# A hybrid attention block: when an attention step makes its rotation tables, applies its keys' weights, and how a sub-norm folds 1/64

## The chip, the cores and the metric

The kernel runs on one core of one Trainium2 chip. The metric is device time in microseconds (us), the median of several executions. TensorE (PE) multiplies matrices, VectorE (DVE) and ScalarE (ACT) do elementwise work, GpSimd (POOL) small elementwise work, and SyncE (SP) issues the DMAs. Each engine works through its own queue in order.

## The reference, cut to what matters

One layer over 2048 tokens: a root-mean-square norm, an input projection, three branches side by side (latent attention with 8 heads, differential attention, attention into 256 memory tokens), a gate and an output projection. The change touches the heads of the latent branch and the sub-norm of the differential branch:

```python
def mla_branch(...):
    q = (rms_norm(cq, q_norm_g) @ w_uq).reshape(b, s, MLA_HEADS, MLA_QK)
    kv = (rms_norm(ckv, kv_norm_g) @ w_ukv).reshape(b, s, MLA_HEADS, MLA_NOPE + MLA_V)
    k_nope, v = kv[..., :MLA_NOPE], kv[..., MLA_NOPE:]
    k = jnp.concatenate([k_nope, k_rope], axis=-1)
    q = rms_norm(q, qn_g)
    k = rms_norm(k, kn_g)
    q = jnp.concatenate([q[..., :MLA_NOPE], rope(q[..., MLA_NOPE:], pos)], axis=-1)
    k = jnp.concatenate([k[..., :MLA_NOPE], rope(k[..., MLA_NOPE:], pos)], axis=-1)
    ...
def diff_branch(...):
    ...
    o = rms_norm(o, subln_g) * (1.0 - lam_init)
```

Here `rms_norm(x, g)` is x / sqrt(mean(x²) + 1e-6) · g; a head of the latent branch has 64 plain and 32 rotated elements.

## The kernel before

The work is cut into steps of 512 tokens (four tiles of 128). There are 4 steps `m` (memory), 8 steps `d` (differential, two groups of heads) and 16 steps `a` (latent, four groups of two heads). Each step has a preparation, which runs while the steps before it still multiply, and its maps: scores on PE, an exponential on ACT (line 506), the rest of it in a second 16-bit part on DVE (`plo`, line 507), and three matmuls per tile with the values (lines 516, 518, 536). A loop at the end of the kernel (lines 1203 to 1238) emits preparations, maps, projections and output tiles by due times written out by hand and gives each piece a priority. A scheduler then fixes each engine's order when the program is built: it plays the program through with its own idea of durations, and whenever an engine is free it takes, of the instructions that are then ready, the one of best priority. A piece that is emitted late can so be placed early, where nothing better is ready. On the chip the order is fixed; an instruction that is not ready holds up all behind it on its engine.

The preparation of an `a` step is `prep_a` (lines 825 to 901). PE projects the latents; ACT copies queries (line 844) and keys (845) to SBUF. ACT squares the keys in two halves (853) and the queries (855), and DVE sums them (854, 857). POOL adds the shared key's sum (861), adds epsilon (97) and raises to -0.5 (101), for queries and keys at once: this is the root, `r`. POOL also rotates the 32 last elements of the queries in place (`rope_in_place`, lines 354 to 358), with tables of cosine and sine times the norm weight that `rope_tabs` makes (four POOL operations, lines 332 to 335) in a buffer of which there is one (`tag="rtab"`, `bufs=1`, line 328). It scales the rotated shared key (866). DVE multiplies the keys by the root (871) and by `g_n`, the product of the two norm weights (872), and the queries by the root (874). ACT and DVE split keys and queries in two 16-bit parts (880, 881 and 886, 887), and SP's queue sends them through transposing DMAs (882 to `kT`, 890 to `qB`). An estimate of the row maxima on PE follows (398), from which the final `qB` is made (899).

The sub-norm of the differential branch is `post_d` (lines 590 to 607). ACT squares eight groups with their sums (596); POOL adds epsilon, takes the root and multiplies by 1/64 (97, 101, 599); DVE multiplies `y` by it (602).

In the kernel before, `prep_a` emits its root and its products so:

```python
        V.reduce_sum(ss[:, 0, :], sq.rearrange(...), axis=AX.X)
        tb = rope_tabs(b, g_q[:, 64:96], nm)
        ...
        V.tensor_tensor(kn[..., 0:64], kn[..., 0:64], _bc(rk, 3, 64), ALU.mult)
        V.tensor_tensor(kn[..., 0:64], kn[..., 0:64], _bc(_bc(g_n, 1, 2), 1, 4), ALU.mult)
        yield 1.0
        V.tensor_tensor(q, q, _bc(rq, 3, 96), ALU.mult)
```

Of the kernel before, what the change touches and what calls it, by code (L numbers as in the profile page):

```python
# [15 lines left out]
AF = mybir.ActivationFunctionType  # L16
ALU = mybir.AluOpType
# [8 lines left out]
EPS = 1e-6  # L26
NEG = -1.0e30
WS = 64.0
# [4 lines left out]
def _bc(ap, axis, n):  # L33
    ap = ap.unsqueeze(axis)
    shape = list(ap.shape)
    shape[axis] = n
    return ap.broadcast_to(shape)
# [3 lines left out]
def hybrid_block(ctx: ExitStack, tc: tile.TileContext, x, mem, positions, norm_g, w_in, mla_q_norm_g,  # L41
# [3 lines left out]
    V, A, G, T, SP = nc.vector, nc.scalar, nc.gpsimd, nc.tensor, nc.sync  # L45
# [37 lines left out]
    def gain_row(src, n, name):  # L83
        t = cst.tile([P, n], F32, name=name)
        SP.dma_start(t, src.broadcast_to([P, n]))
        return t
# [1 line left out]
    gx = gain_cols(norm_g, NK, "gx", WS)  # L88
    gm = gain_cols(mem_norm_g, NK, "gm", WS, G)

    def rstd_of(ss, shape, name, tag="rstd"):
        r = sm.tile([P, 32 if tag == "rstd" else 8], F32, tag=tag, name=name)
        n = int(np.prod(shape))
        rv = r[:, 0:n]
        if len(shape) == 2:
            rv = rv.rearrange("p (a b) -> p a b", b=shape[1])
        G.tensor_scalar(rv, ss, EPS, None, ALU.add)
        m = mhalf
        if len(shape) == 2:
            m = m.unsqueeze(2)  # L100
        G.tensor_tensor(rv, rv, m.broadcast_to([P] + list(shape)), ALU.pow)  # L101
        return rv
# [96 lines left out]
    def new_qkv(name):  # L199
        return wk.tile([P, 4, 256], F32, tag="qkv", name=name, bufs=2)  # L200
# [103 lines left out]
    g_q = gain_row(mla_qn_g, 96, "g_q")  # L304
    g_k = gain_row(mla_kn_g, 96, "g_k")
    g_n = cst.tile([P, 64], F32, name="g_n")
# [19 lines left out]
    def rope_tabs(b, g, name):  # L326

        tb = wk.tile([P, 2, 4, 32], F32, tag="rtab", name=f"rt_{name}", bufs=1)
        c = cos_t[:, 4 * b:4 * b + 4, :]
        s = sin_t[:, 4 * b:4 * b + 4, :]  # L330
        g1, g2 = _bc(g[:, 0:16], 1, 4), _bc(g[:, 16:32], 1, 4)
        G.tensor_tensor(tb[:, 0, :, 0:16], c, g1, ALU.mult)
        G.tensor_tensor(tb[:, 0, :, 16:32], c, g2, ALU.mult)
        G.tensor_tensor(tb[:, 1, :, 0:16], s, g2, ALU.mult)
        G.tensor_tensor(tb[:, 1, :, 16:32], s, g1, ALU.mult)
        return tb
# [202 lines left out]
    def new_ys(ct, b):  # L539
        return wk.tile([P, 2, 4, P], F16, tag="ys", name=f"ys{ct}_{b}", bufs=1)  # L540
# [49 lines left out]
    def post_d(st, y):  # L590
        y8 = y.rearrange("p t h d -> p (t h) d")
        ss = sm.tile([P, 8], F32, tag="yss", name=f"yss_{st.name}")
        ys = new_ys(4 + st.g, st.b)
        sink = ys[:, 0].rearrange("p t k -> p (t k)")
        for i in range(8):
            A.activation(sink[:, 64 * i:64 * i + 64], y8[:, i, :], AF.Square, scale=1.0 / 8.0, accum_out=ss[:, i:i + 1])
        yield 1.0
        r = rstd_of(ss[:, 0:8], [8], f"yr_{st.name}", "rstd_y")
        G.tensor_scalar(r, r, 1.0 / WS, None, ALU.mult)
        yield 1.0  # L600
        yield 1.0
        V.tensor_tensor(y8, y8, _bc(r, 2, 64), ALU.mult)
        yield 1.0
        yf = y.rearrange("p t h d -> p t (h d)")
        V.tensor_tensor(yf, yf, st.z, ALU.mult)
        yield 1.0
        yield from finish(st, yf, 4 + st.g, ys)
# [216 lines left out]

    def prep_a(st):
        g, b, nm = st.g, st.b, st.name
        q = new_qkv(f"qkv_{nm}")[:, :, 0:192].rearrange("p t (h d) -> p t h d", d=96)
        knt = tmp4(f"kn_{nm}")
        kn = knt[:, 0:768].rearrange("p (t h d) -> p t h d", t=4, d=96)
        vt = new_v(b, nm)  # L830
        G.memset(vt[:, :, :, 64:65], WS)
        for t in range(4):
            ps = ps_p.tile([P, 512], F32, tag="pp", name="pp")
            q0, k0 = 192 * g, 256 * g
            first = True
            for c in range(2):
                for hx, hw in ((0, 0), (0, 1), (1, 0)):
                    T.matmul(ps[:, 0:192], lhsT=lat_q[b][:, t, hx, c, :], rhs=wuq[c][:, hw, q0:q0 + 192], start=first,
                             stop=False, skip_group_check=True)
                    first = False  # L840
            for i, (hx, hw) in enumerate(((0, 0), (0, 1), (1, 0))):
                T.matmul(ps[:, 192:448], lhsT=lat_kv[b // 2][:, b % 2, t, hx, :], rhs=wukv[0][:, hw, k0:k0 + 256],
                         start=False, stop=(i == 2), skip_group_check=True)
            A.activation(q[:, t], ps[:, 0:192].rearrange("p (h d) -> p h d", d=96), AF.Copy, scale=1.0 / WS)
            A.activation(kn[:, t, :, 0:64], ps[:, 192:320].rearrange("p (h d) -> p h d", d=64), AF.Copy, scale=1.0 / WS)
            put_v(vt[:, t], ps[:, 320:448].rearrange("p (h d) -> p h d", d=64))
            yield 1.6
        sqt = tmp4(f"sqq_{nm}")
        sq = sqt[:, 0:768].rearrange("p (t h d) -> p t h d", t=4, d=96)
        ss = sm.tile([P, 2, 8], F32, tag="ssa", name=f"ss_{nm}")  # L850
        for i, m in enumerate((sqt, knt)):
            sk = m[:, 768:1024].rearrange("p (t h d) -> p t h d", t=2, d=64)
            A.activation(sk, kn[:, 2 * i:2 * i + 2, :, 0:64], AF.Square, scale=1.0 / math.sqrt(96))
            V.reduce_sum(ss[:, 1, 4 * i:4 * i + 4], sk.rearrange("p t h d -> p (t h) d"), axis=AX.X)
        A.activation(sq, q, AF.Square, scale=1.0 / math.sqrt(96))
        yield 1.0
        V.reduce_sum(ss[:, 0, :], sq.rearrange("p t h d -> p (t h) d"), axis=AX.X)
        tb = rope_tabs(b, g_q[:, 64:96], nm)
        yield 1.0
        s4 = ss[:, 1, :].rearrange("p (t h) -> p t h", h=2)  # L860
        G.tensor_tensor(s4, s4, _bc(ss_kr[b], 2, 2), ALU.add)
        r = rstd_of(ss.rearrange("p a b -> p (a b)"), [16], f"r_{nm}")
        rq = r[:, 0:8].rearrange("p (t h) -> p t h", h=2)
        rk = r[:, 8:16].rearrange("p (t h) -> p t h", h=2)
        yield 1.0
        G.tensor_tensor(kn[..., 64:96], _bc(krot[b], 2, 2), _bc(rk, 3, 32), ALU.mult)
        rope_in_place(q[..., 64:96], tb, 2, G, sqt[:, 768:1024])
        yield 1.0
        yield 1.0
        yield 1.0  # L870
        V.tensor_tensor(kn[..., 0:64], kn[..., 0:64], _bc(rk, 3, 64), ALU.mult)
        V.tensor_tensor(kn[..., 0:64], kn[..., 0:64], _bc(_bc(g_n, 1, 2), 1, 4), ALU.mult)
        yield 1.0
        V.tensor_tensor(q, q, _bc(rq, 3, 96), ALU.mult)
        kT = bigt([P, 2, 4, 2, P], f"kT_{nm}") if b in AB else kvp.tile([P, 2, 4, 2, P], F16, tag="kT", name=f"kT_{nm}")
        st.qs, st.qB = [], []
        for h in range(2):
            ks = stack([P, 4, 2, P], f"ks{h}_{nm}")
            G.memset(ks[:, :, :, 96:128], MS)
            A.activation(ks[:, :, 0, 0:96], kn[:, :, h], AF.Copy)  # L880
            V.tensor_tensor(ks[:, :, 1, 0:96], kn[:, :, h], ks[:, :, 0, 0:96], ALU.subtract)
            SP.dma_start_transpose(kT[:, h].rearrange("p t l k -> p (t l) k"), ks.rearrange("p t l d -> p (t l d)"))
            yield 1.0
            qs = stack([P, 2, 4, P], f"qs{h}_{nm}")
            G.memset(qs[:, :, :, 96:128], 0.0)
            A.activation(qs[:, 0, :, 0:96], q[:, :, h], AF.Copy)
            V.tensor_tensor(qs[:, 1, :, 0:96], q[:, :, h], qs[:, 0, :, 0:96], ALU.subtract)
            st.qs.append(qs)
            st.qB.append(new_qb([P, 2, 4, P], f"qB{h}_{nm}"))
            SP.dma_start_transpose(st.qB[h].rearrange("p l t k -> p (l t) k"), qs.rearrange("p l t d -> p (l t d)"))  # L890
            yield 1.0
        st.kTs = st.prev.kTs + [kT] if b else [kT]
        st.Vs = st.prev.Vs + [vt] if b else [vt]
        yield 1.0
        yield 1.0
        for h in range(2):
            yield from est_block(st, h, 1, lambda m: st.qs[h][:, 0, :, 96], lambda m, t: st.qB[h][0:96, 0, t, :],
                                 lambda m, c, n: st.kTs[c][0:96, h, 0:n, 0, :])
            SP.dma_start_transpose(st.qB[h][:, 0], st.qs[h][:, 0].rearrange("p t d -> p (t d)"))
            ready.add((nm, h))  # L900
            yield 1.0
# [208 lines left out]
    for kind, ng in (("m", 1), ("d", 2), ("a", 4)):  # L1110
        for g in range(ng):
            for b in range(NB):
                st = Step()
# [149 lines left out]
```

## Time and profile before

| | us |
|---|---|
| median of 3 runs | 1380.5 (1380.03 to 1385.78) |
| the profiled execution, its own time | 1382.39 |
| span of the profiled execution (first to last instruction) | 1380.7 |
| mean granted clock of TensorE, share of full speed | 0.983 |

The profile is of one execution. A line of the view by groups gives an engine, the operation's output and inputs, how often it ran, its busy time in us, the mean of one in ns, and the idle time of the engine ahead of it with what ended that. In a timeline a bracket is the idle time of the engine ahead of an instruction and what released it. The view by stretches gives, for each stretch, each engine's busy us with its count of instructions, the granted clock, the share of the DMA engines and GB/s.

### The profile page before, as it was taken

What the parts mean: (1) busy time and instruction counts of PE and PEld (TensorE: products, weight loads), DVE (VectorE), ACT (ScalarE), POOL (GpSimd) and SP (SyncE); (2) the same over time, 40 slices, a digit from 0 to 9 for tenths busy, and PEclk for the clock granted to TensorE, in tenths of its full rate; (3) what the DMA queues carried; (4) which work ended last, traced back from release to release, by engine and by line L of the source; (5) the groups of instructions that cost most, each with busy time, mean ns of one, the idle gap of its engine ahead of it and who ended that gap; (6) DMA issues with size and microseconds to landing.
All of it is one profiled execution on the core that took longest, in us unless ns stands there. A gap on an engine that the chain in (4) does not pass through costs nothing.

```text
span 1380.7 us, 35076 instructions
## 1 busy us (share of the span) xinstructions
PE 1297.6 (94%) x13616; PEld 834.4 (60%) x13616; DVE 1113.6 (81%) x2649; ACT 902.8 (65%) x2163; POOL 353.4 (26%) x549
## 2 busy tenths in 40 slices
PE   5988999999999999999999999999998988999998
PEld 2443556667677767767776656656665665655554
DVE  4657888879888867888998888988898888986745
ACT  6656544687877646786986567766766777774521
POOL 2322132403052233113212233232353333200000
PEclk9999999999999999999999999999999999999999
DMA  7998844323113322447345275446535443275452
GB/s 229 199 210 179 183 109 98 59 59 87 42 24 71 78 38 56 78 115 190 118 98 142 55 147 146 104 93 157 117 70 123 124 96 64 43 149 157 138 192 69
DMA packets 294263, 155.53 MB, mean 113 GB/s; under 512 B 239952, under 2 KB 272848, under 8 KB 294096
## 3 DMA queue, kind: packets, MB, share of 16 engines
q1 hardware_dynamic: 294064, 153.29, 47.1%
q8 instruction: 106, 1.74, 0.5%
q14 instruction: 61, 0.50, 0.1%
q0 software_dynamic: 32, 0.00, 0.0%
HBM read 61.75 MB, written 34.34 MB: 70 GB/s over the span
## 4 chain that ended last, share of the span: by engine, by line
PE 53%; DVE 14%; DMA 10%; POOL 9%; ACT 8%; issue 5%; SPq 1%; ACTq 0%; POOLq 0%; DVEq 0%
PE pp L187 6%; PE pp L188 6%; PE pp L189 6%; PE pe L398 5%; DVE plo L507 4%; PE pv L518 3%; PE pv L516 3%; PE pv L536 3%; PE st L572 3%; PE pp L957 3%; PE pp L958 3%; PE pp L959 3%; POOL r_a L101 2%; PE st L916 2%; PE st L917 2%
## 5 line engine op out<-in xcount | busy, mean ns | idle before, releaser
L506 ACT ACTIVATE p<-st 128x512 f32<-128x512 f32 (+3 forms) x672 | 356.1, 550 | 178.0 <-PE st L918 72.2
L507 DVE TENSOR_TENSOR plo<-p 128x512 f16<-128x512 f32 (+3 forms) x672 | 405.6, 615 | 61.9 <-ACT p L506 58.7
L407 ACT ACTIVATE ec<-pe 128x512 bf16<-128x512 f32 (+3 forms) x384 | 197.6, 536 | 34.1 <-PE pe L400 15.2
L516 PEld LDWEIGHTS <-p 128*128 128x128 bf16 x2304 | 187.0, 99 | 49.3 <-issue 5.1
L518 PEld LDWEIGHTS <-p 128*128 128x128 bf16 x2304 | 173.8, 98 | 41.5 <-issue 4.4
L408 DVE TENSOR_TENSOR er<-er,ec 128x512 bf16<-128x512 bf16 (+3 forms) x384 | 141.0, 377 | 29.9 <-ACT ec L407 15.1
L404 ACT ACTIVATE er<-pe 128x512 bf16<-128x512 f32 x192 | 110.2, 606 | 44.2 <-DVE mx_d L413 14.1
L536 PEld LDWEIGHTS <-plo 128*128 128x128 f16 x2304 | 123.6, 98 | 24.0 <-DVE plo L507 8.6
L916 PE MATMUL st<-qB_a,kT_a 97*128 97x512 f16 (+1 forms) x320 | 112.6, 352 | 19.2 <-ACT p L506 14.3
L189 PEld LDWEIGHTS <-ht_x 128*128 128x128 f16 x896 | 87.8, 98 | 54.8 <-ACT ht_x L137 5.1
L188 PEld LDWEIGHTS <-ht_x 128*128 128x128 f16 x896 | 87.8, 98 | 50.2 <-issue 6.4
L572 PE MATMUL st<-qB_d,kT_d 97*128 97x512 f16 (+1 forms) x320 | 112.2, 355 | 6.0 <-DMA qB_d<-s_d 2.9
L516 PE MATMUL pv<-V_d,p 128*128 128x65 f16 x1088 | 116.4, 194 | 0.8 <-DVE y_d L579 0.8
L187 PEld LDWEIGHTS <-ht_x 128*128 128x128 f16 x896 | 87.8, 98 | 46.6 <-issue 2.9
L518 PE MATMUL pv<-V_d,p 128*128 128x64 f16 x1088 | 115.9, 196 | 0.0
L516 PE MATMUL pv<-V_a,p 128*128 128x65 f16 x1088 | 113.9, 194 | 0.4 <-DVE y_a L923 0.4
L518 PE MATMUL pv<-V_a,p 128*128 128x64 f16 x1088 | 113.2, 196 | 0.0
L917 PE MATMUL st<-qB_a,kT_a 96*128 96x512 f16 (+1 forms) x320 | 112.3, 351 | 0.0
L398 PE MATMUL pe<-kT_d,qB_d 96*128 96x512 f16 (+2 forms) x320 | 106.4, 351 | 6.0 <-ACT ec L407 3.5
L918 PE MATMUL st<-qB_a,kT_a 96*128 96x512 f16 (+1 forms) x320 | 111.6, 349 | 0.0
L398 PE MATMUL pe<-kT_a,qB_a 96*128 96x512 f16 (+2 forms) x320 | 102.4, 353 | 6.6 <-DMA qB_a<-qs_a 3.1
L189 PE MATMUL pp<-w_d,ht_x 128*128 128x512 f16 x256 | 97.0, 379 | 0.0
(294 smaller groups left out, 3356.1 us busy)
## 6 DMA issues: line engine op xcount, KB each, us to landing
xt_x<-in_x_dram SPq DMA_DIRECT2D x16, 512.0 KB, 4.6
xr<-in_x_dram SPq DMA_DIRECT2D x16, 512.0 KB, 3.7
part<-xr SPq DMA_DIRECT2D x16, 512.0 KB, 3.1
ysc<-yt SPq DMA_DIRECT2D x31, 256.0 KB, 2.1
yl<-ysc SPq DMA_DIRECT2D x15, 512.0 KB, 4.4
zsc<-zc SPq DMA_DIRECT2D x48, 128.0 KB, 2.2
xa<-part SPq DMA_DIRECT2D x12, 512.0 KB, 3.6
out_dram<-xa SPq DMA_DIRECT2D x12, 512.0 KB, 3.3
```

The lines of the kernel that those rows point to most:

```text
L187: T.matmul(ps[:, :n], lhsT=ht[:, 0, k], rhs=wt[:, 0, :n], start=(k == 0), stop=False)
L188: T.matmul(ps[:, :n], lhsT=ht[:, 0, k], rhs=wt[:, 1, :n], start=False, stop=False)
L189: T.matmul(ps[:, :n], lhsT=ht[:, 1, k], rhs=wt[:, 0, :n], start=False, stop=(k == NK - 1))
L398: T.matmul(ps[:, 0:n], lhsT=lhs(m, t), rhs=rhs(m, c, n // P), start=True, stop=c < b)
L407: A.activation(ec[:, 0:n], ps[:, 0:n], AF.Copy)
L408: V.tensor_tensor(er[:, t % 2, 0:n], er[:, t % 2, 0:n], ec[:, 0:n], ALU.max)
L506: A.activation(p32[:, :n], ps[:, :n], AF.Exp, scale=self.scale)
L507: V.tensor_tensor(plo[:, :n], p32[:, :n], phi[:, :n], ALU.subtract)
L516: T.matmul(pvv[:, t, 0:65], lhsT=phi[:, c], rhs=vt[:, 0:65], start=(j == 0 and t == 0), stop=False, skip_group_check=True)
L518: T.matmul(pvv[:, t, 0:64], lhsT=phi[:, c], rhs=vt[:, 65:129], start=False, stop=False, skip_group_check=True)
L536: last["pv"] = T.matmul(pvv[:, t, 0:65], lhsT=plo[:, c], rhs=vt[:, 0:65], start=False, stop=(j == self.njt - 1), skip_group_check=True)
L572: T.matmul(ps[:, :n], lhsT=st.kTs[j // 4][0:97, h, j % 4, m % 2, :], rhs=st.qB[h][0:97, t0:4, m % 2, :], start=True, stop=not diag)
```

## The change

A step `a` calls `rope_tabs` as its first act, ahead of its buffers and its projection, where it stood behind the sum of the queries' squares. The product of the keys with `g_n` moves from behind their product with the root to the place that the tables leave, behind the sum of the queries' squares; both products are made in place, so the keys come out the same. (`if 1:` is always taken.) In the sub-norm ACT squares 64/8·y where it squared 1/8·y, epsilon is multiplied by 64² and the operation of line 599 goes: the power -0.5 of 64²·(mean + epsilon) is 1/64 of the root.

```diff
-    def rstd_of(ss, shape, name, tag="rstd"):
+    def rstd_of(ss, shape, name, tag="rstd", eps=EPS):
...
-        G.tensor_scalar(rv, ss, EPS, None, ALU.add)
+        G.tensor_scalar(rv, ss, eps, None, ALU.add)
...
-            A.activation(sink[:, 64 * i:64 * i + 64], y8[:, i, :], AF.Square, scale=1.0 / 8.0, accum_out=ss[:, i:i + 1])
-        yield 1.0
-        r = rstd_of(ss[:, 0:8], [8], f"yr_{st.name}", "rstd_y")
-        G.tensor_scalar(r, r, 1.0 / WS, None, ALU.mult)
+            A.activation(sink[:, 64 * i:64 * i + 64], y8[:, i, :], AF.Square, scale=WS / 8.0, accum_out=ss[:, i:i + 1])
+        yield 1.0
+        r = rstd_of(ss[:, 0:8], [8], f"yr_{st.name}", "rstd_y", EPS * WS * WS)
...
     def prep_a(st):
         g, b, nm = st.g, st.b, st.name
+        tb = rope_tabs(b, g_q[:, 64:96], nm)
...
         V.reduce_sum(ss[:, 0, :], sq.rearrange("p t h d -> p (t h) d"), axis=AX.X)
-        tb = rope_tabs(b, g_q[:, 64:96], nm)
+        V.tensor_tensor(kn[..., 0:64], kn[..., 0:64], _bc(_bc(g_n, 1, 2), 1, 4), ALU.mult)
...
-        V.tensor_tensor(kn[..., 0:64], kn[..., 0:64], _bc(rk, 3, 64), ALU.mult)
-        V.tensor_tensor(kn[..., 0:64], kn[..., 0:64], _bc(_bc(g_n, 1, 2), 1, 4), ALU.mult)
-        yield 1.0
-        V.tensor_tensor(q, q, _bc(rq, 3, 96), ALU.mult)
+        if 1:
+            V.tensor_tensor(kn[..., 0:64], kn[..., 0:64], _bc(rk, 3, 64), ALU.mult)
+        yield 1.0
+        if 1:
+            V.tensor_tensor(q, q, _bc(rq, 3, 96), ALU.mult)
```

## Rows read from the trace of the kernel before

**Rows 1.** The page's first part: busy time of each engine, its share, instructions

```profile
PE 1297.6 (94%) x13616; PEld 834.4 (60%) x13616; DVE 1113.6 (81%) x2649; ACT 902.8 (65%) x2163; POOL 353.4 (26%) x549
```

**Rows 2.** View by stretches: length, busy us per engine, clock, DMA share, GB/s

```profile
400.00:640.00 240.00, 231.25 (x2699) 165.86 (x2697) 197.54 (x513) 165.56 (x433) 73.81 (x101) 0.99 0.35 77
...
680.00:1245.00 565.00, 529.46 (x6086) 350.02 (x6083) 496.11 (x1182) 399.36 (x979) 175.76 (x285) 0.97 0.48 108
```

**Rows 3.** Waits of PE, 640 to 1245 us: total, times, longest

```profile
PE st L916 <- ACT p L506: 14.3, 14, 4.3
...
PE st L916 <- DMA qB_a<-qs_a: 4.2, 3, 2.1
...
PE pv L536 <- DVE plo L507: 3.3, 4, 1.5
...
PE pe L398 <- DMA qB_a<-qs_a: 3.1, 1, 3.1
```

**Rows 4.** Waits of DVE, whole span: total, times, longest

```profile
DVE kn_a L871 <- POOL r_a L101: 16.2, 10, 4.3
...
DVE y_d L602 <- POOL yr_d L599: 6.9, 7, 2.7
```

**Rows 5.** Timeline of DVE at the longest wait: start, length

```profile
1058.66 0.69 DVE L871 TENSOR_TENSOR kn_a<-kn_a,r_a 128x512 f32<-128x512 f32 x1 [4.28 <-POOL r_a L101]
1059.27 1.37 DVE L874 TENSOR_TENSOR qkv_a<-qkv_a,r_a 128x768 f32<-128x768 f32 x1
1060.56 0.68 DVE L507 TENSOR_TENSOR plo<-p 128x512 f16<-128x512 f32 x1
1061.16 0.68 DVE L872 TENSOR_TENSOR kn_a<-kn_a,g_n 128x512 f32<-128x512 f32 x1
```

**Rows 6.** View by stretches, the 5 us after that wait

```profile
1060.00:1065.00 5.00, 3.22 (x33) 2.87 (x33) 5.00 (x10) 3.79 (x10) 0.07 (x1) 0.66 0.26 105
```

**Rows 7.** Groups by line, POOL and DVE

```profile
L332 POOL TENSOR_TENSOR rt_a<-cos_t,g_q 128x64 f32<-128x64 f32 x16 | 7.0, 439 | 0.0
...
L333 POOL TENSOR_TENSOR rt_a<-cos_t,g_q 128x64 f32<-128x64 f32 x16 | 8.5, 529 | 0.0
...
L334 POOL TENSOR_TENSOR rt_a<-sin_t,g_q 128x64 f32<-128x64 f32 x16 | 8.1, 506 | 0.0
...
L335 POOL TENSOR_TENSOR rt_a<-sin_t,g_q 128x64 f32<-128x64 f32 x16 | 7.6, 474 | 0.0
...
L599 POOL TENSOR_SCALAR yr_d<-yr_d 128x8 f32<-128x8 f32 x8 | 2.0, 252 | 0.7
...
L872 DVE TENSOR_TENSOR kn_a<-kn_a,g_n 128x512 f32<-128x512 f32 x16 | 11.0, 685 | 0.0
```

**Rows 8.** Timeline of POOL, first a step and the tables of the second

```profile
634.37 0.32 POOL L332 TENSOR_TENSOR rt_a<-cos_t,g_q 128x64 f32<-128x64 f32 x1
...
679.41 0.94 POOL L354 TENSOR_TENSOR sqq_a<-qkv_a,rt_a 128x128 f32<-128x128 f32 x1 [22.09 <-ACT qkv_a L844]
...
682.92 0.46 POOL L358 TENSOR_TENSOR qkv_a<-qkv_a,sqq_a 128x128 f32<-128x128 f32 x1
683.34 0.32 POOL L332 TENSOR_TENSOR rt_a<-cos_t,g_q 128x64 f32<-128x64 f32 x1
...
684.55 0.60 POOL L861 TENSOR_TENSOR ss_a<-ss_a,sskr 128x8 f32<-128x8 f32 x1
...
688.88 0.61 POOL L866 TENSOR_TENSOR kn_a<-krot,r_a 128x256 f32<-128x256 f32 x1
```

**Rows 9.** Timeline of SP's queue, transposes of one a step

```profile
858.57 1.23 SPq L890 DMA_TRANSPOSE qB_a<-qs_a  x1
860.27 2.78 SPq L882 DMA_TRANSPOSE kT_a<-ks_a  x2
```

**Rows 10.** View of line 874: ns least, median, most

```profile
L874 DVE TENSOR_TENSOR qkv_a<-qkv_a,r_a x16: 944/1371/1373, 690.9 to 1197.7; 128x768 f32<-128x768 f32 x16
```

**Rows 11.** Timeline of POOL beside the line 874 of Rows 5

```profile
1058.70 1.12 POOL L866 TENSOR_TENSOR kn_a<-krot,r_a 128x256 f32<-128x256 f32 x1
```

## The prediction

> **What bounds the kernel now.** I read the page's first part, the view by stretches, the waits of PE and DVE, then timelines of single steps. PE is busy 94% of the span [rows 1], so only what stops PE can be won. The stage of the 16 `a` steps runs from about 680 to 1245 us. There PE is idle 565 - 529.5 = 35.5 us and DVE 565 - 496.1 = 68.9 us, and PE's granted clock averages 0.97 [rows 2]. PE's idle time has two visible causes: the exponentials and their low parts come late (14.3 + 3.3 us), or a transposed query does (4.2 + 3.1 us) [rows 3].
>
> Behind the first cause stands DVE's queue. Ten times of sixteen DVE sits at line 871, the product of the keys with the root, until POOL has the root: 16.2 us, once 4.28 us [rows 4]. All `plo` behind it wait too; ACT runs out of buffers for exponentials, and PE stops. At the longest wait DVE starts line 871 at 1058.66, spends 1.37 us on line 874, and takes the next `plo` only at 1060.56 [rows 5]. PE's longest wait for an exponential, 4.3 us, belongs to this place [rows 3], and PE comes back at a lower clock: 0.66 on average from 1060 to 1065, a mixture of the levels 1.2 and 2.4 GHz [rows 6].
>
> **The tables.** The four operations of a step take 439 + 529 + 506 + 474 ns = 1.95 us [rows 7]. In the code they belong to the step that they serve; the order on POOL is another. The tables of the first `a` step begin at 634.37, 45 us before that step's rotation reads them at 679.41; those of the second come at 683.34, directly behind the first step's rotation and ahead of the first step's sum at 684.55 [rows 8]. The scheduler takes them as soon as their only buffer is free: its last reader is line 356, and what follows of the older step, line 358 at 682.92, goes first [rows 8]; in 13 of the 15 steps that have a next one the tables stand so between lines 358 and 861. So they already run a step ahead, where they delay the older step's root. Emitting them earlier in their own step cannot free the buffer sooner, and everything of the older step still outranks them. I take 0 for the move. It adds no instruction and no DMA, and passes POOL's memsets, the sum and the root of its own step in emission only; SP's queue has nothing of it. Bounds: if tables really left the root's way, ten waits could shrink by 1.95 us each, except that no wait shrinks below zero: at most 16.2 - (4.28 - 1.95) = 13.9 us of DVE. Upwards, a set placed directly ahead of line 354 would delay the rotation by 1.95 us, 16 times 1.95 = 31 us of POOL, of which POOL's idle three quarters [rows 1] should hide nearly all; I allow 2 us.
>
> **The keys' weights.** The product with `g_n` (line 872) takes 0.685 us on DVE, 16 times 11.0 us [rows 7], and remains. It moves from behind the root to behind the sums. There it adds a wait for ACT's second square of the keys, but the sum of that half, ahead of it, waits for the same square; behind it on DVE stand the `plo`, for which PE waits. Its cover in the new place is the root itself: from the sum on POOL at 684.55 to the end of the root at 688.88 are 4.3 us [rows 8]. In ten steps DVE runs dry in this window, so 0.685 us of work is moved into idle time: at most ten times 0.685 = 6.85 us (one of the waits can be shorter than that). How much of it PE sees I take from the stage: 35.5 us of PE's idle time stand against 68.9 us of DVE's [rows 2], about half, so **-3.5 us**. In the other six steps there is no idle time to fill: 0.
>
> The bounds of this term: as gain, the full 6.85 us, and perhaps low clock that follows a stop, 0.34 of 5 us or 1.7 us at a place like [rows 6]; I take none of that. As loss, nothing is excluded: pushed ahead of the root in all 16 steps, the product could cost its own 11.0 us [rows 7]. I take the middle of the gain because the waits are in the trace and the loss is not.
>
> With line 872 gone from behind line 874, the keys are ready when the root's product (0.69 us) and POOL's line 866 are, instead of at 1061.16 + 0.68 [rows 5]: some 2 us earlier. The rest of the preparation fits into the time that PE spends on other steps' maps, and PE's only waits on transposes are for queries [rows 3]. I take 0. If that cover is gone, the queries are late next (second rival).
>
> **The sub-norm.** Line 599 goes: 8 times 252 ns [rows 7]. DVE waited for it 7 times, 6.9 us [rows 4], so at most 7 times 0.25 = 1.8 us of DVE; most of it lies in the `d` steps, where 8.7 us of PE's idle time stand against 42.5 us of DVE's [rows 2], a fifth: **-0.4 us**, between 0 and -1.8. The squares' scale and epsilon are constants of the same instructions: 0.
>
> **The sum.** 0 - 3.5 + 0 - 0.4 = -3.9 us. The profiled execution has a span of 1380.7 us and 1.7 us around it, 1382.4 in all, 1.9 above the median of 1380.5. So its span would be 1376.8, its own time 1378.5, and the median 1376.6 us, a gain of 0.28%. About 0.5%, 6.9 us, is what a measurement of this kernel can tell from no change.
>
> **The rivals.** *The tables do leave the root's way* (chance 0.14). Then 13.9 us of DVE's waits go, half of it PE's: -7; with two low-clock stretches like [rows 6] fewer, -3.4, and the sub-norm, the time is about 1369.5. For it speaks that in 13 steps the tables are what the sum waits behind; against it that the buffer is what places them, and the change leaves it alone.
>
> *The keys overtake the queries* (0.14): the case that ends slower. Today line 874 stands ahead of line 872 [rows 5], so a step's first query transpose is issued first, at 858.57, and the two of the keys at 860.27, 1.39 us each on SP's queue [rows 9]. With the keys ready before line 874 ends, their copies on ACT and their transposes can be put first. An estimate against older blocks needs the query and no new key, so it starts later by 1.4 to 2.8 us. PE already waits for queries four times, 7.3 us [rows 3]; if each grows by 2 us and each such stop brings 1.7 us of low clock, it is 15 us less the 3.9 won: 1391. It decides from the point at which both key transposes stand ahead of the query's in steps where PE has no other maps. Against it: the preparation runs ahead of need in most steps.
>
> *The product costs the root what it saves DVE* (0.08). Line 874 takes 944 ns at best and 1371 in the median [rows 10], and where it takes 1.37 us, at 1059.27, POOL's line 866 with 1.12 us lies beside it [rows 5, 11]: the two slow each other. If the moved product holds up POOL's sum by its 0.685 us in each step, the ten waits grow by what was filled, and six steps lose up to 0.685: from 1380 to 1384.5. The Trainium skill ("SBUF — State Buffer", section "Who interferes with whom") says that a Vector instruction with two SBUF inputs and a GpSimd instruction that reads SBUF exclude each other for a whole instruction; by that rule this rival holds wherever the product starts just ahead of POOL's sum, and the time would be up to 1384.5 where the sum from rows says 1376.6. The durations of line 874 agree with it; but a `plo` has two SBUF inputs too, and stands in that place now.
>
> *PE never saw it* (0.12): DVE's gap is filled, but the stop of PE is ended by the first `plo` behind line 874, whose time stays. Then only the sub-norm counts: 1380.
>
> **How the numbers follow.** The forecast keeps 0.52. Its own range is 1371 to 1381: the gain in full with a low-clock stretch, and none. Any new order of DVE lets the scheduler place later pieces otherwise, and one stop like [rows 5, 6] more or less is 4.3 + 1.7 = 6 us; this widens both sides of every case. For 8 in 10 I reach from 1366 (rival one, a little more) to 1389 (most of the second). Faster by over 0.5% (below 1373.6): nearly all of the first rival, 0.13, and a third of the forecast, 0.16: 0.29. Slower by over 0.5% (above 1387.4): most of the second rival and a little of the third: 0.14. The rest, 0.57, is within 0.5%.
>
> **What the profile after would show.** Tables: POOL's order still has lines 332 to 335 between lines 358 and 861; should they stand elsewhere, the step is wrong. Keys: line 872's successor directly behind the sums, DVE's waits at line 871 down from 16.2 to about 10 us, PE's waits for exponentials down from 14.3 to about 11. Sub-norm: line 599 gone, the waits of line 602 down by under 2 us. Queries: the transposes of line 890 still ahead of those of line 882 and PE's waits for `qB` near 7 us; if they double, the second rival has won. A stop of PE over 3 us in a place with none before would show the order of the whole schedule to outweigh these terms.

## The result and the profile after

The kernel after takes 1372.46 us (median, 1371.28 to 1374.57) beside 1381.91 us of the kernel before in the same comparison: ratio 0.993, 95% interval [0.9912, 0.9948], so 0.7% faster. A second measurement gave 1374.30 us and 0.9943 [0.9929, 0.9956]. The profiled execution has a span of 1369.5 us (own time 1371.28) and a mean clock of 0.986, where before had 1380.7 us and 0.983: 11.2 us less.

The page's first part of the kernel after, for [rows 1]:

```profile
PE 1294.6 (95%) x13616; PEld 831.4 (61%) x13616; DVE 1114.0 (81%) x2649; ACT 900.6 (66%) x2163; POOL 352.6 (26%) x541
```

The count of matmuls is the same, so the difference splits in two: PE is busy 1297.6 - 1294.6 = 3.0 us less (the same matmuls at a somewhat higher granted clock), and idle 83.1 - 74.9 = 8.2 us less.

View by stretches of the kernel after, for [rows 2]:

```profile
400.00:640.00 240.00, 234.50 (x2788) 169.77 (x2786) 202.84 (x527) 166.82 (x437) 67.10 (x97) 0.99 0.37 79
680.00:1245.00 565.00, 534.85 (x6159) 350.02 (x6158) 499.71 (x1193) 399.10 (x982) 177.64 (x271) 0.98 0.49 112
```

PE is busy 3.3 us longer in the first of these stretches and 5.4 us longer in the second, by the same marks of time. The first is surprising: no `a` step computes there, and the only edit that reaches it is that of the sub-norm, with the loss of line 599.

Waits of DVE over the whole span, after, for [rows 4] (line numbers: 871 is now 872, 602 is now 601):

```profile
DVE kn_a L872 <- POOL r_a L101: 20.8, 12, 3.5
...
DVE y_d L601 <- POOL yr_d L101: 1.5, 3, 0.6
```

Waits of PE from 640 to 1245 us, after, for [rows 3]:

```profile
PE st L917 <- ACT p L506: 12.1, 13, 2.8
PE pe L398 <- DMA qB_a<-qs_a: 4.1, 2, 3.1
...
PE pv L536 <- DVE plo L507: 2.2, 3, 1.2
...
PE st L917 <- DMA qB_a<-qs_a: 0.5, 1, 0.5
```

DVE's waits at the root's product have **grown** from 16.2 to 20.8 us, where they should have shrunk to about 10, yet PE waits a little less for exponentials: the longest such stop is 2.8 us, where before has one of 4.3. The rows below show where the moved product went. Timeline of DVE in the kernel after, the step whose wait is the longest:

```profile
837.14 0.95 DVE L857 TENSOR_REDUCE ss_a<-sqq_a 128x8 f32<-128x768 f32 x1 [0.39 <-ACT sqq_a L855]
838.01 0.41 DVE L854 TENSOR_REDUCE ss_a<-kn_a 128x4 f32<-128x256 f32 x1
838.34 0.68 DVE L858 TENSOR_TENSOR kn_a<-kn_a,g_n 128x512 f32<-128x512 f32 x1
...
843.43 0.80 DVE L547 TENSOR_TENSOR ys<-y_a,ys 128x512 f16<-128x512 f32 x1
847.68 0.69 DVE L872 TENSOR_TENSOR kn_a<-kn_a,r_a 128x512 f32<-128x512 f32 x1 [3.46 <-POOL r_a L101]
848.29 1.37 DVE L875 TENSOR_TENSOR qkv_a<-qkv_a,r_a 128x768 f32<-128x768 f32 x1
```

Timeline of POOL beside it:

```profile
841.30 0.64 POOL L358 TENSOR_TENSOR qkv_a<-qkv_a,sqq_a 128x128 f32<-128x128 f32 x1
841.89 0.77 POOL L332 TENSOR_TENSOR rt_a<-cos_t,g_q 128x64 f32<-128x64 f32 x1
...
843.65 0.65 POOL L861 TENSOR_TENSOR ss_a<-ss_a,sskr 128x8 f32<-128x8 f32 x1
844.38 0.26 POOL L97 TENSOR_SCALAR r_a<-ss_a 128x16 f32<-128x16 f32 x1
844.73 2.92 POOL L101 TENSOR_TENSOR r_a<-r_a,mhalf 128x16 f32<-128x16 f32 x1
```

The moved product (line 858) runs at 838.34, directly behind the sums. The root begins only at 844.73, since POOL first works through the rotation, the next step's tables and the sum. So the product does not lie in the gap that DVE leaves at 844.2 to 847.7; it was done five microseconds earlier, and no longer stands behind the root either. That the waits grew for this reason is not shown: below, a version whose product stays in its old place has 20.9 us of them, and one with the product moved has 14.0. The place itself holds in all 16 steps: line 858 starts 2.9 to 7.2 us before its step's root does, and in none of them while the root runs.

The tables stand where they stood ([rows 8]): lines 332 to 335 between lines 358 and 861, again in 13 steps. The queue has changed. Timeline of SP's queue after, transposes of the first `a` step, for [rows 9]:

```profile
686.18 2.62 SPq L883 DMA_TRANSPOSE kT_a<-ks_a  x2
689.51 1.89 SPq L891 DMA_TRANSPOSE qB_a<-qs_a  x1
692.13 1.23 SPq L891 DMA_TRANSPOSE qB_a<-qs_a  x1
```

In before the same step has the queries first (line 890 is 891 after, 882 is 883):

```profile
694.83 2.62 SPq L890 DMA_TRANSPOSE qB_a<-qs_a  x2
697.54 1.31 SPq L882 DMA_TRANSPOSE kT_a<-ks_a  x1
699.56 1.44 SPq L882 DMA_TRANSPOSE kT_a<-ks_a  x1
```

So the keys do overtake the queries, as the slower rival has it, in each of the first six `a` steps; from the seventh on keys often stand first in before as well (at 921.8 and 923.3 us, that step's queries at 937.0 and 944.4). But PE waits for queries less than before: 4.1 + 0.5 = 4.6 us, where [rows 3] have 4.2 + 3.1 = 7.3. Most of it is one stop, in a place where before has none:

```profile
754.66 0.45 PE L398 MATMUL pe<-kT_a,qB_a 96*128 96x512 f16 x2 [3.06 <-DMA qB_a<-qs_a]
```

**The stretch before 640 us.** Timeline of POOL in before, in the last part of a `d` step's sub-norm, and under it that of DVE:

```profile
413.08 4.10 POOL L97 TENSOR_SCALAR yr_d<-yss_d 128x8 f32<-128x8 f32 x1 [0.77 <-ACT ys L596]
417.23 0.56 POOL L462 MEMSET s_d<- 128x256 f16 x2
417.75 1.67 POOL L101 TENSOR_TENSOR yr_d<-yr_d,mhalf 128x8 f32<-128x8 f32 x1
419.51 0.25 POOL L599 TENSOR_SCALAR yr_d<-yr_d 128x8 f32<-128x8 f32 x1
```

```profile
413.04 1.35 DVE L408 TENSOR_TENSOR er<-er,ec 128x512 bf16<-128x512 bf16 x4
...
416.79 0.28 DVE L412 TENSOR_TENSOR er<-er 128x256 bf16<-128x256 bf16 x1
419.80 0.69 DVE L602 TENSOR_TENSOR y_d<-y_d,yr_d 128x512 f32<-128x512 f32 x1 [2.73 <-POOL yr_d L599]
```

PE in before, just behind it:

```profile
421.62 0.30 PE L536 MATMUL pv<-V_d,plo 128*128 128x65 f16 x4 [1.87 <-DVE plo L507]
```

The same place in the kernel after, POOL and DVE:

```profile
412.51 0.56 POOL L462 MEMSET s_d<- 128x256 f16 x2
416.04 0.48 POOL L97 TENSOR_SCALAR yr_d<-yss_d 128x8 f32<-128x8 f32 x1 [2.98 <-ACT ys L596]
416.61 1.81 POOL L101 TENSOR_TENSOR yr_d<-yr_d,mhalf 128x8 f32<-128x8 f32 x1
```

```profile
418.50 0.68 DVE L601 TENSOR_TENSOR y_d<-y_d,yr_d 128x512 f32<-128x512 f32 x1
```

An addition on 128x8 numbers took 4.10 us in before and 0.48 us in after; DVE's 2.73 us at line 602 are gone, and with them the stop of 1.87 us of PE. Line 599 itself is 0.25 us of it. The order around it is another: the memset has moved ahead of line 97, and DVE has another mix beside it.

### The profile page after: what moved, and what is told of

It reads as the page before. It is cut to its first block, busy times and chain, and to the rows that moved or that the text cites. A ratio compares the mean times of both kernels' runs of the same rounds, so it can differ in the third digit from the quotient of the medians.

```text
span 1369.5 us, 35093 instructions
## 1 busy us (share of the span) xinstructions
PE 1294.6 (95%) x13616; PEld 831.4 (61%) x13616; DVE 1114.0 (81%) x2649; ACT 900.6 (66%) x2163; POOL 352.6 (26%) x541
## 4 chain that ended last, share of the span: by engine, by line
PE 64%; DVE 10%; POOL 8%; DMA 7%; ACT 6%; issue 3%; SPq 1%; ACTq 0%; DVEq 0%; POOLq 0%
PE pp L189 7%; PE pp L188 7%; PE pp L187 7%; PE pe L398 6%; PE pv L518 4%; PE pv L516 4%; PE pv L536 4%; PE st L572 3%; PE pp L958 3%; PE pp L960 3%; PE pp L959 3%; DVE plo L507 3%; PE st L917 3%; PE st L918 3%; PE st L919 3%
## 5 line engine op out<-in xcount | busy, mean ns | idle before, releaser
L188 PEld LDWEIGHTS <-ht_x 128*128 128x128 f16 x896 | 87.8, 98 | 47.9 <-issue 3.7
L187 PEld LDWEIGHTS <-ht_x 128*128 128x128 f16 x896 | 87.8, 98 | 47.0 <-issue 2.7
```

The lines of the kernel that those rows point to most:

```text
L187: T.matmul(ps[:, :n], lhsT=ht[:, 0, k], rhs=wt[:, 0, :n], start=(k == 0), stop=False)
L188: T.matmul(ps[:, :n], lhsT=ht[:, 0, k], rhs=wt[:, 1, :n], start=False, stop=False)
```

## The experiments

Two theories. **Parts**: each part of the change costs or saves something of its own, and the parts add. **Order**: what the parts do on their engines is too small to see; the list scheduler turns every edit into another order of the whole schedule, and the order sets the time. Versions below are written against before, and the three parts are called T (tables), K (keys' product) and N (sub-norm). Each ratio is against runs of before that were measured beside the version (medians of 1381.75 to 1382.76 us).

**Each part alone, and the change once more.** T: the call of `rope_tabs` moved. K: the product moved. N: the constant folded.

```diff
T  +        g, b, nm = st.g, st.b, st.name; tb = rope_tabs(b, g_q[:, 64:96], nm)
T  -        tb = rope_tabs(b, g_q[:, 64:96], nm)
K  +        V.reduce_sum(ss[:, 0, :], ...); V.tensor_tensor(kn[..., 0:64], kn[..., 0:64], _bc(_bc(g_n, 1, 2), 1, 4), ALU.mult)
K  -        V.tensor_tensor(kn[..., 0:64], kn[..., 0:64], _bc(_bc(g_n, 1, 2), 1, 4), ALU.mult)
N  -        G.tensor_scalar(r, r, 1.0 / WS, None, ALU.mult)
```

> Only the tables move to the head of the step. The work and the buffer are those of before. Theory of the prediction (the buffer places the tables): the time of before within 3 us, the tables still between lines 358 and 861. Rival (the tables leave the root's way): 7 us or more below before, and the waits of line 871 well under 16.2 us. Rival (any new order of the queues counts by itself): a difference of 2 to 6 us in either direction, though the tables stand where they stood, because the order of later a steps is another.

T: 1381.22 us, ratio 0.999 [0.9979, 1.0001]: no change, as the buffer's theory has it. DVE's waits at the root are 20.9 us all the same, though the product with `g_n` stands where it stood.

> Only the product with the norm weights moves ahead of the root. Theory of the prediction (it fills DVE's idle time at the root): 3.5 us below before, the waits for the root down to about 10 us. What the trace of the changed kernel says against it: those waits grew to 20.8 us there, in 12 places; if that is this part's doing, the waits are near 20 us here too, and the gain, if any, comes from fewer and shorter stops of PE behind them. Rival (order by itself): between 5 us below and 5 us above before.

K: 1398.58 us, ratio 1.0114 [1.0099, 1.0128], 16.8 us slower, where the rival of order allowed 5.

> Only 1/64 goes under the sub-norm's root: one POOL operation of 0.25 us less in each of 8 d steps. Theory of the prediction: 0.4 us below before. Theory from the changed kernel's trace: it runs some 6 us ahead of before at the first a step's tables (628.4 against 634.4 us), where neither of the other parts has acted, so this part alone brings 4 to 7 us. Rival (order by itself): it is ahead at that point and the lead is lost or doubled later by another order of the a steps.

N: 1378.20 us, ratio 0.9969 [0.9957, 0.9982], 3.5 us faster: more than the prediction's 0.4, a little under the 4 to 7 read from the trace.

> The changed kernel once more, on the chip of the three parts: 8 to 10 us below before. If the parts add, the three differences sum to this.

The whole change: 1374.30 us, ratio 0.9943 [0.9929, 0.9956]. The parts' sum is 0 + 16.8 - 3.5 = +13 us, the whole -7.5 us. They don't add.

K is the clearest look at what the moved product does. Its busy line on the page, then its waits of PE from 640 to 1245 us:

```profile
PE 1309.5 (94%) x13616; PEld 838.3 (60%) x13616; DVE 1115.2 (80%) x2649; ACT 901.7 (65%) x2163; POOL 358.9 (26%) x549
```

```profile
PE st L916 <- ACT p L506: 11.3, 11, 3.4
PE pe L398 <- DMA qB_a<-qs_a: 8.6, 5, 3.0
PE pv L536 <- DVE plo L507: 8.0, 4, 3.1
...
PE st L916 <- DMA qB_a<-qs_a: 0.4, 1, 0.4
```

Against before ([rows 1, 3]) PE is busy 11.9 us longer with the same 13616 matmuls and idle 88.2 - 83.1 = 5.1 us longer. More than two thirds of the loss are longer matmuls, and most of that is the lower clock: an estimate from the mean clocks of 0.976 and 0.983 gives 0.024 x 1397.7 - 0.017 x 1380.7 = 10 us. Of the waits, those for low parts grew by 4.7 us and those for queries at line 398 by 5.5, but at line 916 those for queries fell from 4.2 to 0.4: for queries in all, 9.0 us where before has 7.3. SP's queue in K and in before, second `a` step:

```profile
742.60 2.61 SPq L882 DMA_TRANSPOSE kT_a<-ks_a  x2
745.31 1.23 SPq L899 DMA_TRANSPOSE qB_a<-qs_a  x1
746.63 1.27 SPq L890 DMA_TRANSPOSE qB_a<-qs_a  x1
...
762.04 1.24 SPq L890 DMA_TRANSPOSE qB_a<-qs_a  x1
```

```profile
735.28 1.23 SPq L890 DMA_TRANSPOSE qB_a<-qs_a  x1
737.24 2.61 SPq L882 DMA_TRANSPOSE kT_a<-ks_a  x2
```

The keys go first, the query 4.0 us behind them, and PE stops at the estimates that need the step's queries. Timeline of PE in K:

```profile
751.55 0.71 PE L398 MATMUL pe<-kT_a,qB_a 96*128 96x512 f16 x2 [2.96 <-DMA qB_a<-qs_a]
...
766.45 0.45 PE L398 MATMUL pe<-kT_a,qB_a 96*128 96x512 f16 x2 [2.61 <-DMA qB_a<-qs_a]
```

The first of these stops is what the slower rival described. The second waits for the step's other query, which the queue sends only at 762.04, some 17 us after it is through with the keys: it is not the keys that hold it up. The loss of 16.8 us is near the 15 that the rival gave to late queries, but the waits for queries did not double, which was its sign. Whether the overtaking is the *cause* of the loss is the next question.

**Queries written first.** In `prep_a` the queries' product, copies and transposes are put ahead of the keys', in K and in the kernel after:

```diff
-        V.tensor_tensor(kn[..., 0:64], kn[..., 0:64], _bc(rk, 3, 64), ALU.mult)
+        V.tensor_tensor(q, q, _bc(rq, 3, 96), ALU.mult)
...
-        V.tensor_tensor(q, q, _bc(rq, 3, 96), ALU.mult)
+        V.tensor_tensor(kn[..., 0:64], kn[..., 0:64], _bc(rk, 3, 64), ALU.mult)
...
         for h in range(2):
+            qs = stack([P, 2, 4, P], f"qs{h}_{nm}")
...
             ks = stack([P, 4, 2, P], f"ks{h}_{nm}")
```

> The kernel before with the keys' product alone moved (that alone took 1398.6 us, 16.8 us more than before), and in prep_a the queries' product, copies and transposes written ahead of the keys'. Theory A (the moved product made the keys' copies and transposes overtake the queries'; TensorE waits for query transposes 18.8 us in place of 11.2): with the queries written first these waits fall to 11 us or less and the time comes back to 1378 to 1388 us. Theory B (the 16.8 us are the order of the whole schedule, in which the queries' lateness is only one of many shifted places): the waits for query transposes may fall, but the time doesn't follow them and may lie anywhere from 1372 to 1400 us; at 1390 us or more A is out.

1387.98 us, ratio 1.0046 [1.0028, 1.0063]. In the first six `a` steps a query now goes first, as in before. The time falls by 10.6 us and lies just inside theory A's bounds; but the waits of everything that reads `qB` in `a` steps are 17.5 us in 12 places, where K has 18.8 in 12 and before 11.2 in 7. These figures, here and in the expectations, add the waits of matmuls and of weight loads, so most stops count twice; on matmuls alone, over the whole span, they are 8.9, 9.4 and 7.3 us. They hardly fell, so they are not what came back.

> The kernel after with the queries' product, copies and transposes written ahead of the keys'. In the kernel after the keys' transposes come first as well, and TensorE waits 10.0 us in 7 places for query transposes. Theory A: these waits fall by half or more, and the time falls to 1364 to 1370 us. Theory B: no tie; 1366 to 1390 us, and where it is slower, waits for key transposes or for exponentials have taken their place.

1384.67 us, ratio 1.0015 [0.9999, 1.0032]: here the waits for queries did fall, from 10.0 to 7.0 us (matmuls alone: 4.6 to 3.3), if not by half, and the time *rose* by 10 to 12 us above the two measurements of the kernel after. The same reversal wins 10.6 us in K and loses as much in the kernel after, and the time does not follow the waits for queries; theory A, in which they carry the loss, is out.

**Pairs of parts.** K and N without T:

> The change without its part on the tables. If the parts added, it would take 1381.8 + 16.8 - 3.5 = 1395 us. If the tables cost and save nothing where they stand (the part alone measured 0) and what counts is the keys' and the norm's part together, it takes as long as the whole change, 1370 to 1376 us. If the tables' place is what turns the keys' loss into a gain, it stays at 1385 to 1398 us.

1377.90 us, ratio 0.9963 [0.9949, 0.9976], outside all three ranges that were set for it. T and N without K:

> The change without its part on the keys. If the keys' part costs 16.8 us whatever stands beside it, this version lies that much under the whole change: 1355 to 1360 us. If the parts' own costs are near zero and the order decides, 1370 to 1390 us.

1387.67 us, ratio 1.0035 [1.0017, 1.0052]: the part that cost 16.8 us alone here saves some 13 to 15 us when it is added (the two measurements of the whole change against T and N). T and K come from the kernel after with one multiply by 1.0 put back behind the sub-norm's root, which makes the scheduler give all five engines the order of T and K without N, instruction by instruction:

```diff
         r = rstd_of(ss[:, 0:8], [8], f"yr_{st.name}", "rstd_y", EPS * WS * WS)
+        G.tensor_scalar(r, r, 1.0, None, ALU.mult)
```

> The kernel after with one GpSimd multiply (by 1.0) put back behind the sub-norm's root, where line 599 stood in before. With it every engine's order up to 640 us is that of before again, and the whole order that of the tables' and the keys' parts without the norm's. If the norm's part saved the time of an instruction on the way to the multiply of y_d (line 602 of before), this one costs 0.4 to 3.5 us: 1373 to 1376 us. If the gain of the change hangs on the order of the whole schedule, the lead of 3 us at the fifth and sixth differential steps (431 to 480 us of the span) is gone, what follows is another order again, and the time lies anywhere in 1370 to 1400 us; 1395 us or more would say that the keys' part costs its 17 us in every order but that of the whole change.

1389.68 us, ratio 1.0042 [1.0025, 1.0058]. Eight instructions of 0.25 us that do nothing make the kernel after some 14 to 17 us slower.

Now every combination has a ratio, in thousandths from before: T -1.0, K +11.4, N -3.1, TK +4.2, TN +3.5, KN -3.7, TKN -7.0 (-5.7 in the second measurement). By their intervals a difference of two of them is good to some 2 to 3. The worth of a part, with nothing beside it, with one of the other two and with both:

| part | alone | beside T, K or N | beside both others |
|---|---|---|---|
| T | -1.0 | -7.2 (K), +6.6 (N) | -3.3 |
| K | +11.4 | +5.2 (T), -0.6 (N) | -10.5 |
| N | -3.1 | +4.5 (T), -15.1 (K) | -11.2 |

Each changes its sign: none of them has a worth of its own on the whole time that these runs could tell.

**No part at all.** If order is the cause, an edit without any of the change should do as much. First the kernel before with *more* work, a second multiply by 1.0 behind line 599:

```diff
-        G.tensor_scalar(r, r, 1.0 / WS, None, ALU.mult)
+        G.tensor_scalar(r, r, 1.0 / WS, None, ALU.mult); G.tensor_scalar(r, r, 1.0, None, ALU.mult)
```

> The kernel before with one more GpSimd multiply (by 1.0) behind line 599: the suspected cost of the norm's part doubled. If line 599's own duration and place are what the norm's part saved (3.5 us for 8 instructions, of which only 0.4 us were forecast), a second one costs as much again: 1384 to 1387 us. If it is its 0.4 us of time on the path of line 602 alone, 1381.5 to 1383 us. If the norm's gain comes from the new order from 255 us on, the time bears no relation to it: outside 1381 to 1387 us, to either side, as a new order of the whole schedule gives it.

1370.16 us, ratio 0.9906 [0.9882, 0.9929]: 12 us *faster* for eight useless instructions, the fastest version of all. Its interval overlaps that of the kernel after, so it isn't shown to beat it. Its page has PE busy least of all:

```profile
PE 1289.8 (94%) x13616; PEld 828.5 (61%) x13616; DVE 1110.2 (81%) x2649; ACT 901.2 (66%) x2163; POOL 356.6 (26%) x557
```

Then two versions that have the same instructions as before and only another order; one number of the program that orders the emission differs in each:

```diff
-    EP = 200
+    EP = 196
```

> The kernel before with the priority offset of the preparations at 196 in place of 200: no instruction is added, taken away or changed, only the list scheduler's order, from TensorE's row 968 of 27234 on. If the order by itself moves the time by as much as the parts did, it differs from before by 3 us or more, to either side (1365 to 1378 or 1386 to 1400 us). If an order near this one is worth nothing, 1380 to 1384 us, and then the parts' times are their own.

1373.46 us, ratio 0.993 [0.9905, 0.9955]: the gain of the whole change, to the digit, without any of it. PE idles 1371.7 - 1296.6 = 75.1 us in it, as in the kernel after (74.9), while DVE's waits at the root stand at 18.5 us:

```profile
PE 1296.6 (95%) x13616; PEld 831.8 (61%) x13616; DVE 1111.6 (81%) x2649; ACT 901.1 (66%) x2163; POOL 349.2 (25%) x549
```

```profile
DVE kn_a L871 <- POOL r_a L101: 18.5, 14, 3.8
```

```diff
-    FP = 150
+    FP = 154
```

> As the run before it, with the offset of the fill work at 154 in place of 150: the same instructions, another order from TensorE's row 2361 on. The same expectation: beyond 3 us to either side if the order by itself moves the time, else 1380 to 1384 us.

1379.01 us, ratio 0.9971 [0.9954, 0.9988], 3.75 us faster: over the 3 us that were set, by little.

**All profiles side by side**, sorted by span. "Root" is DVE's wait at the product with the root, "queries" PE's wait for `qB` in `a` steps, with matmuls and weight loads added as above. Each line is one execution: the two of the kernel after differ by 4.5 us, and that of "after, queries first" lies 4 us under its version's median:

| version | span, us | PE busy | PE idle | clock | root | queries |
|---|---|---|---|---|---|---|
| one more multiply | 1367.3 | 1289.8 | 77.5 | 0.992 | 21.0 | 11.1 |
| after | 1369.5 | 1294.6 | 74.9 | 0.986 | 20.8 | 10.0 |
| EP 196 | 1371.7 | 1296.6 | 75.1 | 0.986 | 18.5 | 15.3 |
| after, second measurement | 1374.0 | 1295.5 | 78.5 | 0.984 | 22.0 | 10.4 |
| FP 154 | 1376.9 | 1295.9 | 81.0 | 0.985 | 21.6 | 10.4 |
| K and N | 1377.9 | 1294.5 | 83.4 | 0.984 | 14.0 | 18.6 |
| N | 1378.0 | 1298.6 | 79.4 | 0.982 | 14.1 | 17.8 |
| after, queries first | 1379.0 | 1295.2 | 83.8 | 0.985 | 15.0 | 7.0 |
| before | 1380.7 | 1297.6 | 83.1 | 0.983 | 16.2 | 11.2 |
| T | 1381.4 | 1298.2 | 83.2 | 0.985 | 20.9 | 12.0 |
| T and K | 1386.0 | 1298.2 | 87.8 | 0.985 | 17.3 | 17.0 |
| T and N | 1386.6 | 1302.0 | 84.6 | 0.982 | 23.3 | 16.0 |
| K, queries first | 1390.2 | 1303.1 | 87.1 | 0.979 | 20.5 | 17.5 |
| K | 1397.7 | 1309.5 | 88.2 | 0.976 | 19.7 | 18.8 |

The two waits on which the prediction was built do not sort the versions: the shortest waits at the root (14.0 and 14.1) belong to kernels in the middle, and the fastest has one of the longest. These waits grew in T and in FP 154 as well, which leave the product where it was, and shrank in K and N, which moves it. Long waits for queries go loosely with slow versions (the four slowest have 16.0 to 18.8 us), but K and N has 18.6 and is faster than before.

**Where the versions part.** DVE multiplies 64 blocks of outputs, 128x256 each, by the reciprocal of their row sums (lines 579, 686 and 923); in order of time, these are marks along the schedule. Start in before, and how much later (+) or earlier (-) the same mark starts in others:

| mark | before, us | after | T | K | N | KN | TK | TN | EP 196 | FP 154 |
|---|---|---|---|---|---|---|---|---|---|---|
| 22nd | 387.05 | +0.8 | +1.9 | +0.1 | -0.4 | +1.4 | -0.6 | -0.8 | -0.7 | +3.2 |
| 24th | 479.01 | -2.9 | +2.9 | +0.9 | -4.1 | -2.3 | -1.4 | -4.5 | -2.9 | -0.6 |
| 32nd | 771.84 | -4.0 | +1.8 | +10.0 | +0.6 | -1.8 | +8.2 | -1.6 | +1.7 | +7.7 |
| 36th | 842.52 | -2.7 | +1.8 | +20.0 | -0.6 | -3.3 | +17.7 | -0.3 | +1.2 | +7.8 |
| 46th | 1039.05 | -5.2 | -6.3 | +20.9 | -17.1 | +3.1 | +11.6 | -1.0 | -10.3 | -3.3 |
| 60th | 1241.30 | -11.1 | -0.2 | +15.7 | -3.9 | -3.3 | +4.6 | +5.8 | -9.0 | -6.0 |

The second profile of the kernel after has -0.5, -4.2, -2.0, -0.1, -2.7 and -6.5 at these marks, up to 4.6 us from the first: so much lies between two executions of one order.

One difference is steady. From the 22nd to the 24th mark all four versions with N win 3.7 us against before, to the tenth (and so do the second profile of the kernel after and the one with queries first); those without (T, K, TK) lie between -0.9 and +0.9. That is the place of the 4.10 us of line 97. But FP 154 wins 3.7 us there and EP 196 2.2 us, with line 599 in them, and in EP 196 line 97 still takes 3.85 us. The version with one more multiply wins 13.7 us there, after it has come 10.6 us late to the 22nd mark. So another order does as much without N, it is not shown that the instruction does it, and the long line 97 is at most a part of it. It is the one effect of the change that stayed the same whatever stood beside it. Behind it, in the `a` steps, each version goes its own way by up to 21 us at these marks, and N's lead of 4 us can be lost by the 32nd mark.

## Why the prediction was right and wrong

It gave 1376.6 us and a range from 1366 to 1389; 1372.46 lies in the range, 4 us below the number. Its likeliest class, within 0.5%, with 0.57, did not come; faster by over 0.5% had 0.29.

- **Tables, 0**: right in both halves. They stand between lines 358 and 861 as before, and alone the part measures 0.999 [0.9979, 1.0001]. The first rival, which had them leave the root's way, fell with that.
- **Keys' product, -3.5**: the step that failed is "in ten steps DVE runs dry in this window, so 0.685 us of work is moved into idle time". The product goes ahead of the root in all 16 steps, none fills the gap, and alone the part costs 16.8 us. The waits grew from 16.2 to 20.8 us where 10 were forecast, but that the product's place did it is not shown: T alone has 20.9, K and N 14.0. I had taken the window from the sum on POOL (line 861) to the root's end, but DVE may begin the product as soon as its own sums are through, and POOL still has the rotation and four tables before line 861. A list scheduler fills a gap only with what becomes ready in it. The product was ready before. With that the rival in which DVE's gap is filled and PE doesn't see it fell as well.
- **Keys ready earlier, 0, with the queries late next**: the overtaking came, in the kernel after as in K, and the sign "the transposes of line 890 still ahead of line 882" was wrong. So was the reading that before sends a query first: it does so in the first six steps, not in all. No such price was paid: in the kernel after PE's waits for queries are 4.6 us against 7.3 ("near 7" was the sign), and in the runs with the queries written first the time does not follow these waits.
- **The product costs the root what it saves DVE**: partly so, at another instruction. In the rows above the product does not stand ahead of POOL's sum but some 5 us earlier (838.34 against 843.65), beside the rotation, which stands ahead of the sum on POOL; in two steps it does start 0.16 and 0.17 us ahead of the sum. In seven steps it starts up to 0.24 us ahead of the rotation's line 358, which takes 903 to 962 ns there; its seven quickest in before take 452 to 462. The rule of the Trainium skill on shared ports ("SBUF — State Buffer", section "Who interferes with whom") agrees with that. What it costs the whole no run here separates.
- **Sub-norm, -0.4**: mis-sized. It measured -3.5 us alone, 3.7 us of it between two marks around 400 to 480 us. DVE's waits at that multiply fell by 6.9 - 1.5 = 5.4 us (3.8 in the second profile), not by "under 2". The order around it changed, a 4.10 us instruction among it; line 599's 0.25 us is the least of that.
- **The last sentence of the signs** named what decided: the order of the whole schedule outweighs the terms. Its sign came, too, as the stop of 3.06 us at 754.66. The error was to hold this as a widening of 6 us. Versions without the change, or with useless work added, lie 3.75, 9.3 and 12 us from before, against a sum of terms of 3.9. The forecast's centre came out right in sign by luck rather than by its steps: +16.8 and -3.5 alone make +13.

What stays open: which of the new neighbours in the `a` steps makes one order 20 us better than another. The runs show that it is not either of the two waits tabled here, and that by the estimate above a lower clock makes up more than half of the worst loss; what brings the clock down in one order and not in another was not tried.

## What to carry to other kernels

Where a list scheduler orders the engines, time one or two versions that change only the order (a priority, a due time) before a gain below about 1% is given to an edit: here such versions moved by up to 0.7%, and one with useless work by 0.9%. Before counting on a moved instruction to fill a wait, find when its inputs are ready; if that is ahead of the wait, the scheduler runs it there and the wait is not filled. And try each part both alone and taken out of the whole: a part that changes sign between the two has shown no worth of its own.

## What the runs showed of the hardware

GpSimd's addition on 128x8 numbers (line 97, sub-norm) took 4.10 us in five profiles whose order up to there is that of before (before, T, K, T and K, K with queries first) and 3.85 us with EP 196; in the kernel after it took 0.48 us and with FP 154 0.27. In before DVE ran through operations of two inputs back to back beside it, from 413.04 to 417.07, and line 97 ended at 417.18. The same holds wherever line 97 took over 2 us on 128x8 or 128x4 numbers, 16 times in 12 of the 14 profiles (2.36 to 4.10 us): beside it DVE ran two-input operations without a gap, and line 97 ended 0.09 to 0.11 us after the last of them. In the kernel after DVE was as busy, but had gaps of about 0.05 us ahead of and behind the operation at 416.47, and line 97 took its 0.48 us there. The Trainium skill's section named above says that such an operation and GpSimd shut each other out of the shared port, and these rows agree with it; here the small instruction waited for the whole run of operations. That DVE's run is the cause was not tried by itself. The reverse shows in before, too: DVE's line 874 (128x768) took 1368 to 1373 ns in the 11 steps in which POOL's line 866 lay beside its start, and 944 to 947 in the four with nothing on POOL beside it.

The same 13616 matmuls kept TensorE busy from 1289.8 to 1309.5 us, at mean granted clocks from 0.992 down to 0.976. In the slowest version the longer matmuls are 11.9 of 17.0 us lost against before: a sum that prices only the idle time of PE leaves out most of what a bad order costs.
